# Keeping a block inverse by columns: a DeltaNet mixer's 32x32 inversion on VectorE, and what its copy-out holds

## The chip, the cores and the metric

One core of one Trainium2 chip runs the whole program. The metric is the device time of one execution in microseconds (us), median over runs of the same kernel.

## The reference, cut to what matters

The program is a two-layer decoder trunk on 512 tokens of width 1024. Each layer is a SwiGLU half step, a token mixer and another SwiGLU half step. Layer 0's mixer (the "even" one) joins eight sliding-window attention heads with four gated DeltaNet heads; layer 1's is a Mamba-2 scan. The change touches the DeltaNet heads alone. Per chunk they need a unit lower triangular solve:

```python
a_mat = jnp.where(strict, jnp.einsum('bnhid,bnhjd->bnhij', k_beta, kc) * decay, 0.0)
t_mat = a_mat + jnp.eye(B_CHUNK, dtype=a_mat.dtype)
u = lax.linalg.triangular_solve(t_mat, vc * bc, left_side=True, lower=True, unit_diagonal=True)
w = lax.linalg.triangular_solve(t_mat, k_beta * jnp.exp(g_cum)[..., None], ...)
```

(`g_cum` stands here for the cumulated log decay.) All is float32.

## The kernel before, in words

**Matrix products** are the bulk. A float32 product is made of three TensorE passes over parts split in two (high and low): lines L167, L168 and L169 for the projections of the even mixer, so 24 matmuls of 128x512 for one projected tile of 128 columns (8 steps of depth by 3). They gather in one of two PSUM banks of the tag `mm`. The weights of one such tile come by a DMA (L85, on SyncE), are cast by ScalarE (`whi`, L80) and their rest is taken by VectorE (`wlo`, L81).

**The even mixer** (`even_mixer`) runs two generators against each other: `gated_delta` (the DeltaNet heads) and `attention`, whose steps are drawn in between as filling. A scheduler that sorts by program order and readiness then fixes one order of instructions for each engine, and on the chip each engine works through its list in that order. In `gated_delta` the order of the program is: `keys` for four heads, the first half of `invert32`, `queries` for four heads, the second half of `invert32`, `values` for four heads, then the chain that puts the 32x32 blocks together (L769 to L779, on the tiles `U`, `kT` and `h`), and the recurrence.

**The inversion** (`invert32`, L695 to L727) inverts 64 blocks of 32x32 (four on the diagonal of each of 16 matrices), which go through DRAM scratch `ablk` so that each of the 128 partitions holds one block and builds 16 columns of its inverse. `nb` is the negated block (a buffer of the tag `U`, of which there are two, each 128x1024), `tb` the inverse as it grows (one of the two buffers of the tag `feat`), `pr` a scratch for products. Forward substitution takes 31 steps; step i is a VectorE product (L720) of n times m elements and a VectorE sum over m (L721), with n = min(i, 16) and m = i up to 15 and i + 1 from 16 on. Each needs the one before it. In `nb` two neighbours in m lie 32 floats apart, and in `tb` 16 floats apart. At the end one DMA writes `tb` to DRAM scratch `tblk` (L722), and eight DMAs bring the blocks back in place, into `h` (L725).

**The values** (`values(h)`, L729) take one projected tile in an `mm` bank and put it through `conv_silu`: ScalarE's copy with a factor out of PSUM (L474), three VectorE steps that still read the `mm` bank (L478), ScalarE's tanh into a scratch (L480), VectorE's last product (L481). TensorE then transposes the result (L645), and VectorE scales it (L731). The tile on which L474 to L481 work has the tag `feat`.

**The scratch**: `self.scratch()` draws from one pool with the tag `scr` and two buffers of 128x512 float32. `pr`, the tanh outputs of `conv_silu`, the DMA'd rows in `queries` and others draw from it. A buffer is given again when its last reader is done, in the order of the requests in the program.

**Attention**: the score products of a block of 128 queries (L833, L834 into a `tr` bank), VectorE's masked maximum (L838), ScalarE's exponential (L840), VectorE's reciprocal (L841), ScalarE's scaling (L842), TensorE's transposes (L849), the split (`PTh` by ScalarE, `PTl` by VectorE, L80 and L81), for each head eight products with the values (L855), a copy (L858) and a sum (L860).

Of the kernel before, what the change touches and what calls it, by code (L numbers as in the profile page):

```python
# [13 lines left out]
AF = mybir.ActivationFunctionType  # L14
OP = mybir.AluOpType
# [15 lines left out]
class Trunk:  # L31
# [542 lines left out]
    def even_mixer(self, w_in, conv_w, a_log, dt_bias, head_norm_w, w_out, post_w, next_pre):  # L574
        nc, tc = self.nc, self.tc
# [6 lines left out]
        tt, stt = nc.vector.tensor_tensor, nc.vector.scalar_tensor_tensor  # L582
        with ExitStack() as ctx:
# [52 lines left out]
            def t4(name, bufs=HB):  # L636
                return gp.tile([128, TT, 128], F32, name=name, bufs=bufs)

            def two(name):
                return gp.tile([128, 2 * TT, 128], F32, name=name, bufs=2)  # L640
# [54 lines left out]
            def invert32():  # L695


                nb = two("U").rearrange("p a b -> p (a b)").rearrange("p (j i) -> p j i", i=32)
                tb = t4("feat", 2).rearrange("p c t -> p (c t)").rearrange("p (i c) -> p i c", c=16)
                ablk = self.dram.tile([4, HB * TT, 32, 32], F32, name="ablk")  # L700
                tblk = self.dram.tile([2, 4, HB * TT, 32, 16], F32, name="tblk")
                for b in range(4):
                    s = slice(32 * b, 32 * b + 32)
                    nc.sync.dma_start(ablk[b].rearrange("q j i -> j q i"), AT[s, :, s])
                nc.gpsimd.memset(Tm, 0.0)
                nc.gpsimd.memset(tb, 0.0)
                for e in range(2):
                    half = slice(64 * e, 64 * e + 64)
                    nc.sync.dma_start(nb[half], ablk.rearrange("b q j i -> (b q) j i"))
                    nc.gpsimd.memset(tb[half, 16 * e:16 * e + 16, :].rearrange("p a b -> p (a b)")[:, ::17], 1.0)  # L710
                yield
                pr = self.scratch()
                nc.scalar.activation(nb, nb, AF.Copy, scale=-1.0)

                nc.gpsimd.memset(nb.rearrange("p a b -> p (a b)")[:, 16 * 33::33], 1.0)
                for i in range(1, 32):
                    n, m = min(i, 16), i + (i >= 16)
                    q = pr[:, :n * m].rearrange("p (c m) -> p c m", c=n)
                    a = nb[:, :m, i:i + 1].rearrange("p m o -> p o m").to_broadcast([128, n, m])
                    tt(q, a, tb[:, :m, :n].rearrange("p m c -> p c m"), op=OP.mult)  # L720
                    nc.vector.tensor_reduce(tb[:, i, :n], q, axis=mybir.AxisListType.X, op=OP.add)  # L721
                nc.sync.dma_start(tblk.rearrange("e b q i c -> (e b q) i c"), tb)  # L722
                for e in range(2):
                    for b in range(4):
                        nc.sync.dma_start(Tm[32 * b:32 * b + 32, :, 32 * b + 16 * e:32 * b + 16 * e + 16],  # L725
                                          tblk[e, b].rearrange("q i c -> i q c"))
                yield  # L727
# [24 lines left out]
            def gated_delta():  # L752
                heads = range(HB)
                K = []
                for h in heads:
                    K.append(keys(h, first[h]))
                    yield 4
                inv = invert32()
                next(inv)
                Q = []  # L760
# [467 lines left out]
```

## Time and profile before

| what | value |
|---|---|
| runs | 2144.21, 2144.45, 2148.64 us; median 2144.45 us |
| the profiled execution | 2145.76 us, of which the span of its instructions is 2144.0 us |
| mean granted TensorE clock | 0.998 |
| TensorE (PE) | 2108.8 us busy, 98% of the span |
| VectorE (DVE) | 1472.2 us busy, 69% |
| ScalarE (ACT) | 1042.0 us busy, 49% |
| GpSimd (POOL) | 149.4 us busy, 7% |
| the inversion, first product to last sum | 487.74 to 551.44 us in the span |

An engine's busy time says how much of the span it has instructions in work; where TensorE is at 98%, the time is the sum of its work and of the few places where it stands. Such a place is told by a row's bracket, "[1.94 <-DVE h L860]": 1.94 us without work before this instruction, ended by VectorE's write of `h` in line 860. Busy time at a lower granted clock is busy time as well, so the clock is read beside it.

### The profile page before, as it was taken

The numbers are of one execution on the slowest core, as the hardware profiler recorded it, in microseconds if no ns is written. First come the engines' busy times: TensorE is split into PE (matmuls) and PEld (weight loads), VectorE is DVE, ScalarE is ACT, GpSimd is POOL, SyncE is SP. The second block draws the span as 40 slices with busy tenths as digits, with TensorE's granted clock in tenths as the row PEclk, the third lists the DMA queues.
The fourth block names the chain that finished last, engine by engine and source line by source line (L and its number), as shares of the span: only waits on it lengthen the run. The fifth ranks groups of instructions, "written<-read, shape, count | busy, mean of one in ns | idle before, by whom it ended". The sixth has DMA issues, their size and how long they took to land.

```text
span 2144.0 us, 33124 instructions
## 1 busy us (share of the span) xinstructions
PE 2108.8 (98%) x13311; PEld 1869.5 (87%) x13311; DVE 1472.2 (69%) x2329; ACT 1042.0 (49%) x1613; POOL 149.4 (7%) x142
## 2 busy tenths in 40 slices
PE   8999999999999999999999999999999999999998
PEld 7999988887788999988899998887778788999986
DVE  5867656869667776656686765668888846867653
ACT  4555543555563455544345554357565423555541
POOL 0011000111200011000001000000000000011000
PEclk9999999999999999999999999999999999999999
DMA  8587324442323587533657742333333236587321
GB/s 236 145 199 163 124 95 133 109 119 68 94 70 118 148 201 176 135 128 99 158 136 184 172 128 99 101 84 100 108 108 101 78 118 157 141 197 162 122 91 67
DMA packets 284037, 277.06 MB, mean 129 GB/s; under 512 B 18576, under 2 KB 244552, under 8 KB 283884
## 3 DMA queue, kind: packets, MB, share of 16 engines
q1 hardware_dynamic: 243308, 228.81, 35.2%
q0 software_dynamic: 40576, 46.14, 12.8%
q8 instruction: 104, 1.70, 0.3%
q14 instruction: 49, 0.40, 0.1%
HBM read 265.93 MB, written 4.79 MB: 126 GB/s over the span
## 4 chain that ended last, share of the span: by engine, by line
PE 86%; DVE 6%; ACT 3%; DMA 3%; issue 2%; POOL 0%; SPq 0%; DVEq 0%; ACTq 0%; POOLq 0%
PE mm L300 19%; PE acc L300 14%; PE acc L236 10%; PE acc L235 10%; PE acc L237 10%; PE mm L167 4%; PE mm L168 4%; PE mm L169 4%; DMA M<-rows_o 2%; PE acc L651 1%; PE acc L169 1%; PE acc L168 1%; PE acc L167 1%; PE tr L154 1%; DVE wlo L81 1%
## 5 line engine op out<-in xcount | busy, mean ns | idle before, releaser
L80 ACT CAST whi<-wraw 128x1024 fp32r<-128x1024 f32 x296 | 310.1, 1049 | 392.8 <-PE acc L237 116.6
L81 DVE TENSOR_TENSOR wlo<-wraw,whi 128x1024 fp32r<-128x1024 f32 x292 | 356.8, 1223 | 154.9 <-ACT whi L80 153.1
L167 PE MATMUL mm<-uhi,whi 128*128 128x512 f32 (+1 forms) x712 | 264.7, 373 | 2.1 <-DVE feat L478 1.3
L168 PE MATMUL mm<-ulo,whi 128*128 128x512 f32 (+1 forms) x712 | 262.7, 369 | 0.3 <-DVE ulo L81 0.3
L169 PE MATMUL mm<-uhi,wlo 128*128 128x512 f32 (+1 forms) x712 | 262.9, 369 | 0.0
L80 ACT CAST whi<-wq 128x1024 fp32r<-128x1024 f32 x144 | 150.8, 1049 | 223.3 <-issue 83.2
L81 DVE TENSOR_TENSOR wlo<-wq,whi 128x1024 fp32r<-128x1024 f32 x144 | 175.2, 1220 | 83.7 <-ACT whi L80 83.6
L235 PE MATMUL acc<-whi,hs 128*128 128x512 f32 x576 | 227.3, 395 | 0.0
L236 PE MATMUL acc<-wlo,hs 128*128 128x512 f32 x576 | 227.2, 395 | 0.0
L380 POOL DMA_DIRECT2D wq<-in_ffn_w_up_dram x72 | 92.7, 1291 | 1071.0 <-DVE wlo L81 316.6
L300 PE MATMUL mm<-ulo,whi 128*128 128x256 f32 x576 | 163.0, 283 | 0.0
L300 PE MATMUL mm<-uhi,wlo 128*128 128x256 f32 x576 | 163.0, 283 | 0.0
L300 PE MATMUL mm<-uhi,whi 128*128 128x256 f32 x576 | 163.0, 283 | 0.0
L300 PE MATMUL acc<-uhi,whi 128*128 128x256 f32 x576 | 162.8, 283 | 0.0
L300 PE MATMUL acc<-uhi,wlo 128*128 128x256 f32 x576 | 162.8, 283 | 0.0
L300 PE MATMUL acc<-ulo,whi 128*128 128x256 f32 x576 | 162.8, 283 | 0.0
L167 PEld LDWEIGHTS mm<-uhi,whi 128*128 128x128 f32 x712 | 134.5, 189 | 27.8 <-issue 4.2
L168 PEld LDWEIGHTS mm<-ulo,whi 128*128 128x128 f32 x712 | 134.8, 189 | 23.5 <-issue 4.1
L169 PEld LDWEIGHTS mm<-uhi,wlo 128*128 128x128 f32 x712 | 134.7, 189 | 22.9 <-issue 3.4
L237 PE MATMUL acc<-whi,hs 128*128 128x512 f32 x384 | 151.5, 395 | 0.0
L236 PEld LDWEIGHTS acc<-wlo,hs 128*128 128x128 f32 x576 | 108.5, 188 | 25.3
L235 PEld LDWEIGHTS acc<-whi,hs 128*128 128x128 f32 x576 | 108.5, 188 | 25.1
(394 smaller groups left out, 5296.8 us busy)
## 6 DMA issues: line engine op xcount, KB each, us to landing
wraw<-in_ffn_w_down_dram SPq DMA_DIRECT2D x88, 512.0 KB, 3.5
wq<-in_ffn_w_gate_dram SPq DMA_DIRECT2D x72, 512.0 KB, 5.3
wq<-in_ffn_w_up_dram POOLq DMA_DIRECT2D x72, 512.0 KB, 8.1
wraw<-in_ffn_w_gate_dram SPq DMA_DIRECT2D x52, 512.0 KB, 6.2
wraw<-in_ffn_w_up_dram SPq DMA_DIRECT2D x52, 512.0 KB, 6.9
wraw<-in_odd_w_in_dram SPq DMA_DIRECT2D x40, 512.0 KB, 3.9
wq<-in_ffn_w_up_dram SPq DMA_DIRECT2D x36, 512.0 KB, 3.8
wraw<-in_even_w_in_dram SPq DMA_DIRECT2D x28, 512.0 KB, 4.2
```

The costliest lines, as they stand in the source:

```text
L80: nc.scalar.copy(hi, src)
L81: (nc.gpsimd if on_pool else nc.vector).tensor_tensor(lo, src, hi.bitcast(F32), op=OP.subtract)
L154: nc.tensor.transpose(p[:, j * 128:(j + 1) * 128], u[:, k * 128:(k + 1) * 128], self.ident)
L167: nc.tensor.matmul(p, whi[:, k, :], hi, start=k == 0, stop=False)
L168: nc.tensor.matmul(p, whi[:, k, :], lo, start=False, stop=False)
L169: nc.tensor.matmul(p, wlo[:, k, :], hi, start=False, stop=k == KD - 1)
L235: nc.tensor.matmul(p, ahi, hi, start=k == 0, stop=False)
L236: nc.tensor.matmul(p, ahi, lo, start=False, stop=False)
L237: nc.tensor.matmul(p, alo, hi, start=False, stop=k == nk - 1)
L300: self.nc.tensor.matmul(p[:, f * 256:(f + 1) * 256].rearrange("p (t c) -> p t c", c=128), l, r, start=new and f == k == i == 0, stop=f == ...
L380: nc.gpsimd.dma_start(raw, src, accum_op=OP.add)
L651: nc.tensor.matmul(p[:, c, :], lhs[:, c, :], rhs[:, c, :], start=True, stop=True)
```

## The change

In `invert32` the block is read from DRAM into a first `U` buffer `na`; ScalarE's negation (L713 before, L715 after) reads it transposed and writes `nb`, the second `U` buffer, so that m runs contiguously in it. `tb` keeps the inverse by columns (c, then i), so m runs contiguously there too, and the sums are written 32 floats apart. Before the DMA to `tblk` the inverse is brought back into rows by a ScalarE copy (new L724) into a new tile `out`, drawn from `self.scratch()`. Lines behind L697 are 1 to 3 higher in the changed kernel.

```diff
-                nb = two("U").rearrange("p a b -> p (a b)").rearrange("p (j i) -> p j i", i=32)
-                tb = t4("feat", 2).rearrange("p c t -> p (c t)").rearrange("p (i c) -> p i c", c=16)
+                na = two("U").rearrange("p a b -> p (a b)").rearrange("p (j i) -> p j i", i=32)
+
+                nb = two("U").rearrange("p a b -> p (a b)").rearrange("p (i j) -> p i j", j=32)
+                tb = t4("feat", 2).rearrange("p c t -> p (c t)").rearrange("p (c i) -> p c i", i=32)
...
-                    nc.sync.dma_start(nb[half], ablk.rearrange("b q j i -> (b q) j i"))
-                    nc.gpsimd.memset(tb[half, 16 * e:16 * e + 16, :].rearrange("p a b -> p (a b)")[:, ::17], 1.0)
+                    nc.sync.dma_start(na[half], ablk.rearrange("b q j i -> (b q) j i"))
+                    nc.gpsimd.memset(tb[half].rearrange("p c i -> p (c i)")[:, 16 * e::33], 1.0)
                 yield
                 pr = self.scratch()
-                nc.scalar.activation(nb, nb, AF.Copy, scale=-1.0)
+                nc.scalar.activation(nb, na.rearrange("p j i -> p i j"), AF.Copy, scale=-1.0)
 
                 nc.gpsimd.memset(nb.rearrange("p a b -> p (a b)")[:, 16 * 33::33], 1.0)
                 for i in range(1, 32):
                     n, m = min(i, 16), i + (i >= 16)
                     q = pr[:, :n * m].rearrange("p (c m) -> p c m", c=n)
-                    a = nb[:, :m, i:i + 1].rearrange("p m o -> p o m").to_broadcast([128, n, m])
-                    tt(q, a, tb[:, :m, :n].rearrange("p m c -> p c m"), op=OP.mult)
-                    nc.vector.tensor_reduce(tb[:, i, :n], q, axis=mybir.AxisListType.X, op=OP.add)
-                nc.sync.dma_start(tblk.rearrange("e b q i c -> (e b q) i c"), tb)
+                    tt(q, nb[:, i:i + 1, :m].to_broadcast([128, n, m]), tb[:, :n, :m], op=OP.mult)
+                    nc.vector.tensor_reduce(tb[:, :n, i], q, axis=mybir.AxisListType.X, op=OP.add)
+                out = self.scratch().rearrange("p (i c) -> p i c", c=16)
+                nc.scalar.copy(out, tb.rearrange("p c i -> p i c"))
+                nc.sync.dma_start(tblk.rearrange("e b q i c -> (e b q) i c"), out)
```

The change moves instructions on three engines. ScalarE's list before, at the first of the four values' tanh (L480), with the attention's steps around it:

```order
L80 CAST PTh<-tr 128x4x128
L842 ACTIVATE P<-P,aden 128x128
L480 ACTIVATE scr<-feat 128x512
L80 CAST whi<-wraw 128x1024
L858 COPY P<-tr 64x512
L474 ACTIVATE feat<-mm,cw 128x512
L80 CAST PTh<-tr 128x128
L840 ACTIVATE P,aden<-P,amax 128x256
```

ScalarE's list in the changed kernel, at the new copy L724 (`scr<-feat` is `out<-tb`):

```order
L845 ACTIVATE P<-P,aden 128x512
L80 CAST PTh<-tr 128x4x128
L861 COPY P<-tr 64x512
L724 COPY scr<-feat 128x512
L480 ACTIVATE scr<-feat 128x512
L474 ACTIVATE feat<-mm,cw 128x512 x2
L480 ACTIVATE scr<-feat 128x512 x2
L80 CAST whi<-wraw 128x1024
```

The first tanh of the values stood ahead of two more attention blocks; it now stands right behind the copy L724, and the others behind it. VectorE's list before, at the first value's last product (L481):

```order
L720 TENSOR_TENSOR scr<-U,feat 128x49
L115 TENSOR_TENSOR rs_t<-rs_y 128x16
L481 SCALAR_TENSOR_TENSOR feat<-scr,feat 128x512
L721 TENSOR_REDUCE feat<-scr 128x7
L116 TENSOR_TENSOR rs_t<-rs_t,rs_x 128x16
L720 TENSOR_TENSOR scr<-U,feat 128x64
```

VectorE's list in the changed kernel, at the inversion's end:

```order
L721 TENSOR_TENSOR scr<-U,feat 128x496
L722 TENSOR_REDUCE feat<-scr 128x16
L721 TENSOR_TENSOR scr<-U,feat 128x512
L722 TENSOR_REDUCE feat<-scr 128x16
L481 SCALAR_TENSOR_TENSOR feat<-scr,feat 128x512
L478 SCALAR_TENSOR_TENSOR feat<-mm,cw,feat 128x511
L478 SCALAR_TENSOR_TENSOR feat<-mm,cw,feat 128x510
L734 TENSOR_TENSOR vt<-acc,kl 128x512
```

The product L481 stood between step 7's product and sum; it now stands behind the last sum. TensorE's list before, at the first value's transposes (L645), with a score product ahead of them and a projection behind:

```order
L855 MATMUL tr<-PTl,va 128x128
L833 MATMUL tr<-k_4862,q_4766 128x256
L834 MATMUL tr<-k,q 128x256
L645 MATMUL acc<-ident,feat 128x128 x4
L167 MATMUL mm<-uhi,whi 128x512
L168 MATMUL mm<-ulo,whi 128x512
```

TensorE's list in the changed kernel, at the same transposes:

```order
L836 MATMUL tr<-k_4863,q_4767 128x512
L837 MATMUL tr<-k,q 128x512
L852 MATMUL tr<-ident,P 128x128 x7
L858 MATMUL tr<-PTh,va 128x512
L858 MATMUL tr<-PTl,va 128x512
L858 MATMUL tr<-PTh,va 128x384
...
L645 MATMUL acc<-ident,feat 128x128 x4
L167 MATMUL mm<-uhi,whi 128x512
L168 MATMUL mm<-ulo,whi 128x512
```

The transposes of the first value have moved behind the rest of this attention head (three more score blocks, all transposes and the products with the values) and behind the 24 matmuls of the third value's projection, which followed it before.

## Rows read from the trace of the kernel before

**Rows 1.** The page's busy times: engine, us, share of the span, instructions.
```profile
PE 2108.8 (98%) x13311; PEld 1869.5 (87%) x13311; DVE 1472.2 (69%) x2329; ACT 1042.0 (49%) x1613; POOL 149.4 (7%) x142
```

**Rows 2.** Busy time by stretch: us, each engine's busy time (instructions), granted clock, DMA.
```profile
500.00:520.00 20.00, 17.35 (x83) 13.02 (x82) 19.10 (x45) 9.77 (x19) 1.48 (x1) 1.00 0.19 52
520.00:540.00 20.00, 19.18 (x120) 16.90 (x119) 19.87 (x31) 5.83 (x9) 2.70 (x2) 1.00 0.45 124
540.00:560.00 20.00, 17.69 (x93) 14.01 (x92) 16.48 (x35) 10.46 (x24) 4.26 (x3) 1.00 0.40 95
```

**Rows 3.** TensorE's waits from 498 to 700 us: us in total, times, longest.
```profile
PE tr L849 <- ACT P L842: 2.3, 1, 2.3
PE tr L849 <- DVE h L860: 1.9, 1, 1.9
PE mm L167 <- DVE feat L478: 1.3, 2, 0.7
PE acc L651 <- ACT kT L776: 0.6, 1, 0.6
```

**Rows 4.** VectorE's groups from 487 to 552 us: busy us, mean ns | idle before.
```profile
L720 DVE TENSOR_TENSOR scr<-U,feat 128x1 f32<-128x1 f32 (+30 forms) x31 | 18.7, 604 | 0.2
L721 DVE TENSOR_REDUCE feat<-scr 128x1 f32<-128x1 f32 (+30 forms) x31 | 12.4, 399 | 0.2
L478 DVE SCALAR_TENSOR_TENSOR feat<-mm,cw,feat 128x511 f32<-128x511 f32 (+2 forms) x12 | 8.9, 738 | 0.0
L81 DVE TENSOR_TENSOR wlo<-wraw,whi 128x1024 fp32r<-128x1024 f32 x7 | 8.5, 1217 | 0.0
L838 DVE CUSTOM_DVE_ANT_0 P<-tr,abias 128x384 f32<-128x384 f32 (+3 forms) x8 | 3.8, 478 | 0.8 <-PE tr L834 0.8
L81 DVE TENSOR_TENSOR PTl<-tr,PTh 128x256 fp32r<-128x256 f32 (+3 forms) x7 | 3.6, 512 | 0.2 <-ACT PTh L80 0.2
L119 DVE TENSOR_TENSOR rs_y<-rs_t,rs_y 128x16 f32<-128x16 f32 x1 | 2.2, 2204 | 0.0
```

**Rows 5.** VectorE's timeline at two products and sums: start us, us [idle before].
```profile
498.86 0.27 DVE L720 TENSOR_TENSOR scr<-U,feat 128x64 f32<-128x64 f32 x1
499.17 0.22 DVE L721 TENSOR_REDUCE feat<-scr 128x8 f32<-128x64 f32 x1
...
549.42 1.03 DVE L720 TENSOR_TENSOR scr<-U,feat 128x512 f32<-128x512 f32 x1
...
550.76 0.68 DVE L721 TENSOR_REDUCE feat<-scr 128x16 f32<-128x512 f32 x1
```

**Rows 6.** ScalarE's timeline: the first tanh and a copy.
```profile
497.35 0.62 ACT L480 ACTIVATE scr<-feat 128x512 f32<-128x512 f32 x1
...
562.18 0.58 ACT L858 COPY P<-tr 64x512 f32<-64x512 f32 x1 [2.13 <-PE tr L855]
```

**Rows 7.** VectorE's timeline, the first value's last product.
```profile
498.03 0.68 DVE L481 SCALAR_TENSOR_TENSOR feat<-scr,feat 128x512 f32<-128x512 f32 x1
```

**Rows 8.** TensorE's timeline: the first value's transposes, attention's transposes, projections.
```profile
499.60 0.66 PE L645 MATMUL acc<-ident,feat 128*128 128x128 f32 x4
...
515.76 0.93 PE L849 MATMUL tr<-ident,P 128*128 128x128 f32 x7
...
519.89 0.48 PE L167 MATMUL mm<-uhi,whi 128*128 128x512 f32 x1
...
523.40 0.39 PE L855 MATMUL tr<-PTh,va 128*128 128x512 f32 x1
...
524.50 0.27 PE L855 MATMUL tr<-PTl,va 128*128 128x128 f32 x1
```

**Rows 9.** Busy time and granted clock around two places where TensorE stood.
```profile
417.40:419.90 2.50, 0.19 (x2) 0.00 (x0) 2.50 (x3) 2.11 (x9) 1.86 (x1) 1.00 0.74 171
419.90:424.00 4.10, 4.06 (x21) 4.06 (x22) 3.81 (x21) 0.00 (x0) 0.00 (x0) 0.58 0.93 236
...
500.00:503.00 3.00, 1.18 (x7) 0.66 (x5) 2.90 (x5) 0.69 (x1) 1.48 (x1) 1.00 0.07 9
```

## The prediction

> **What bounds the kernel now.** I read the page's busy times first. TensorE is busy for 2108.8 of 2144.0 us [rows 1], so VectorE's 1472 us only count where TensorE stands waiting for it. Then the stretch of the inversion by twenties: VectorE is full there (19.10 and 19.87 of 20 us), yet TensorE still does 17.35 and 19.18 of 20 [rows 2]. TensorE's waits from 498 to 700 us are 2.3, 1.9, 1.3 and 0.6 us, 6.1 in all [rows 3], and no wait on a product or sum of the inversion is among them. So the inversion (18.7 us of products, 12.4 us of sums, spread over 64 us [rows 4]) lies beside other work, and making it shorter can return no more than those 6.1 us. What counts is what the change does to the orders that TensorE, ScalarE and VectorE work through.
>
> **Part 1, the layout (a gain for VectorE).** In before a sum, whose input is contiguous, takes 0.22 us for 64 elements and 0.68 for 512; a product takes 0.27 and 1.03 [rows 5]. That is 1.03 ns an element on 0.155 us for the contiguous form, and 1.70 ns an element for the strided one. A contiguous VectorE operation with two inputs agrees: 1024 elements in 1.217 us [rows 4] against 1.21 by this line. I price the new products at the contiguous line. The reads gain (1.70 - 1.03) ns an element. The sums now write 16 results 128 bytes apart; the trace shows no such write, the nearest is the strided product's surcharge of 0.67 ns, times 16 is 0.01 us a sum, so I take nothing (upper bound 31 times 0.01 = 0.3 us). The Trainium skill ("SBUF — State Buffer", Door 1, the note on cachelines) says that each access that crosses to a new 16-byte line pays a penalty. By that the strided products are dear, as rows 5 show, but the new scattered sums and the copy's strided read pay too, which speaks against this change; it would leave my sum as it stands, since both are inside the bounds given here.
>
> **Part 2, the new scratch (the step that decides).** `out` comes from the two-buffer pool `scr`. `pr` holds one buffer for the whole inversion. Before, the other one went round among the values' tanh outputs, and so the first L480 ran at 497.35 us [rows 6], L481 at 498.03 [rows 7], TensorE's transposes at 499.60 [rows 8], in the middle of the inversion. Now `out` is asked for ahead of the values, takes that other buffer, and is written only when the inversion is over. All four tanh outputs come behind it. The orders show it: L480 right behind the copy L724 on ScalarE, L481 behind the last sum on VectorE. TensorE works in order, and its transposes L645 stand behind only what is left of one attention head and one projection. The values that have been projected hold both `mm` banks, so no projection can stand ahead of them either.
>
> When does the inversion end? Up to 498.0 us I leave the course as it is, with seven steps done. Steps 8 to 31 have 1100 + 6272 = 7372 elements in the products and as many in the sums: 14744 times 1.03 ns is 15.2 us, 48 times 0.155 is 7.4, and the 0.04 us between a product's end and its sum's start (499.13 to 499.17 [rows 5]) 48 times is 1.9: 24.5 us. Attention's and the queries' remaining VectorE work falls in between: three maxima at 0.48, four `PTl` at 0.51, two L860 of the 0.68 us of a 128x512 operation (as L481 [rows 7]), a `wlo` at 1.22, the slow L119 at 2.2 [rows 4] and some 0.8 us of small ones: 9.0, of which I take 8.0 as added, since neighbours that don't depend on each other overlap a little. So it ends at 498.0 + 24.5 + 8.0 = 530.5 us, 21 earlier than before's 551.4. Then come the copy, L480 and L481, one after the other. The copy L724 is new: its lower bound is a contiguous ScalarE copy, 0.58 us [rows 6]; its upper bound that of a tanh of 0.62 us stretched as strided products are, 1.03/0.68, so 0.94. I take 0.65, near the copy. With 0.62, 0.68 and 0.15 for hand-overs, L645 starts at 532.6 us.
>
> What does TensorE do from about 501.0, where it first stands in before as well, to 532.6? By its order: 18 products at (523.40 - 519.89)/15 = 0.234 us, 4.2; ten transposes at 0.93/7, 1.3; eight products with the values, 523.40 to 524.77, 1.4; four score products at the 0.39 of a 512-wide one, 1.6 [rows 8]; 0.3 for changes between them. That is 8.8 of 31.6 us: **22.8 us idle**.
>
> **Part 3, what is late next.** Behind these transposes stands the last value's projection, and it needs an `mm` bank, free only after the second value's three L478: 3 times 0.738 [rows 4] is 2.2, with a hand-over **2.3 us**. The projections of the last value, of `q` and `k` then run on end, but attention's fill has been spent, so the chain that joins the blocks is covered thinly: each of the four heads may show the wait of 0.6 us for ScalarE's `kT` [rows 3], so 0 to 2.4, and I take **2.0**. The last attention head has no other work beside it at its end. Before, one link of such a head stood bare for 2.3 us [rows 3], so one to four links cost 2.3 to 9.2 us; I take two and 0.9 for the rest, **5.5**. The DMAs to `tblk` and back into `h` start 20 us earlier than before and no one waits for them.
>
> **Part 4, TensorE's clock.** Where TensorE stood at 417.4 to 419.9 (0.19 us of work in 2.50), the granted clock was 0.58 in the next 4.1 us, part of them at the lower level, 1.2 GHz; where it stood about 1.9 us at 501 to 503, it stayed at 1.00 [rows 9]. A loss is therefore 4.1 times 0.42 = 1.7 us where it comes. Idle of 22.8 us in pieces, and a tail, may give none to four of those (0 to 7 us); I take two, **3.4 us**.
>
> **The sum.** Idle 22.8 + 2.3 + 2.0 + 5.5 = 32.6, less the 6.1 of before that this stretch takes up, plus 3.4: +29.9 us. The profiled execution took 2145.76 us (span 2144.0), 1.3 above the median of the runs; with the change it would take 2175.7, and a run by the median 2144.45 + 29.9 = **2174.4 us**.
>
> **Rivals.**
> - *Faster: VectorE's relief reaches TensorE.* If the tanh outputs don't queue behind `out` (were a third buffer free in time), the inversion's shorter operations let L860 and L478 come sooner, and the 6.1 us of waits go: 2144.45 - 6.1 = 2138.3 us. It decides from the point where L645 starts before TensorE has run through its 8.8 us, at about 510. For it speaks that VectorE is full there [rows 2]; against it, the three orders, and an inversion that can't end before 522 even without other work. 4 in 100, with 2 in 100 for a half of it that can't be told from no change (0.2%, 4.3 us, is about what a measurement of this kernel can tell).
> - *The layout doesn't do what it says.* If a broadcast operand, not the stride, makes products slow, the 7372 elements stay at 1.70 ns: 4.9 us later, 2179.3 us. For it: both versions broadcast one operand, and no product of before is contiguous. Against: the slope of 1.70 has no counterpart in other two-input operations. 12 in 100.
> - *The clock stays low.* If TensorE, after so long a stop and with work in pieces, is at 0.58 not for 4 but for some 25 us more, it loses 25 times 0.42 = 10.5 us: 2184.9 us. For it, the row at 419.9; against it, the row at 500, where the clock stayed at 1.00 through the stop, and the projections of 24 matmuls each that run on end soon after L645. 10 in 100. The Trainium skill ("TensorE: Matmul & The Clock Gate", Part 1) calls the throttled clock the default, which activity releases; by that, thin work in the stop would keep it low for longer, which is this case, and the row at 0.58 agrees so far.
> - *Later parts give it back.* If the chain and the tail stay covered by the projections and by next weights' work, 2.0 and 5.5 go, and one clock loss: 2174.4 - 9.2 = 2165.2 us. 10 in 100.
>
> **How the numbers follow.** The forecast itself has 62 in 100, with 2168 to 2180 from its bounds (copy +0.3, tail -3.2 to +3.7, clock -3.4 to +3.6, chain -2.0 to +0.4, not all at one end). The range takes in later parts that give back, with a shorter tail, down to 2160, and the low clock up to 2187; outside lie the faster rival and the ends of these, some 15 in 100. Faster by over 0.2%: 0.04; within: 0.02; slower: 0.94.
>
> **What would show it.** Right: L724 behind the last sum at about 530, L645 at about 532 with over 10 us of TensorE's idle ended by VectorE's `feat` of L481; a product of 512 at about 0.69 us; the stretch 500 to 540 with some 24 us less TensorE work than before. Wrong: L480 while the inversion runs; a product of 512 still at 1.03; a TensorE stop that ends with another releaser, or a time below 2155 us, which would mean that TensorE had work which I haven't seen in its order.

## The result, and the profile after

The changed kernel takes 2184.93 us (median of 4 runs, 2183.19 to 2187.97) against 2144.7 us before: a ratio of 1.0178, with a 95% interval from 1.0167 to 1.019. That is 40.2 us slower, inside the range that was forecast (2160 to 2187), 10.5 us above the forecast of 2174.4 and above the 2168 to 2180 that the forecast's own bounds gave. The profiled execution is the one of 2183.19 us, with a span of 2181.4, 37.4 us above before's 2144.0.

The page's busy times of the changed kernel, as in [rows 1]:

```profile
PE 2117.4 (97%) x13311; PEld 1873.1 (86%) x13311; DVE 1473.3 (68%) x2329; ACT 1044.8 (48%) x1614; POOL 148.9 (7%) x142
```

TensorE does the same 13311 matmuls. It is busy 8.6 us longer (2117.4 - 2108.8), and its idle time, the span less the busy time, is 64.0 us instead of 35.2: 28.8 more. The two make up the 37.4. VectorE's total is no smaller either: its groups add up to some 3 us less (1564.8 against 1568.1), but fewer of its instructions overlap now.

TensorE's waits of the changed kernel from 480 to 740 us, as in [rows 3]:

```profile
PE acc L645 <- DVE feat L481: 17.3, 1, 17.3
PE tr L852 <- ACT P L845: 6.6, 3, 2.4
PE mm L198 <- DVE q L81: 2.0, 1, 2.0
PE mm L167 <- DVE feat L478: 1.8, 1, 1.8
PE tr L852 <- DVE h L863: 1.7, 1, 1.7
PE tr L858 <- ACT PTh L80: 1.4, 2, 0.7
PE tr L925 <- DVE h L863: 1.2, 1, 1.2
PE tr L852 <- DVE amax L841: 1.0, 1, 1.0
```

One wait of 17.3 us stands at the top: the first value's transposes L645 for VectorE's L481. How it comes about is read from three timelines of the changed kernel, VectorE's, ScalarE's and TensorE's (columns as in [rows 5]):

```profile
530.80 0.69 DVE L721 TENSOR_TENSOR scr<-U,feat 128x512 f32<-128x512 f32 x1
531.53 0.69 DVE L722 TENSOR_REDUCE feat<-scr 128x16 f32<-128x512 f32 x1
533.93 0.69 DVE L481 SCALAR_TENSOR_TENSOR feat<-scr,feat 128x512 f32<-128x512 f32 x1 [1.71 <-ACT scr L480]
```

```profile
532.30 1.06 ACT L724 COPY scr<-feat 128x512 f32<-128x512 f32 x1 [14.36 <-DVE feat L722]
533.27 0.62 ACT L480 ACTIVATE scr<-feat 128x512 f32<-128x512 f32 x1
```

```profile
516.91 0.41 PE L858 MATMUL tr<-PTl,va 128*128 128x128 f32 x1
534.67 1.11 PE L645 MATMUL acc<-ident,feat 128*128 128x128 f32 x4 [17.34 <-DVE feat L481]
537.58 0.77 PE L167 MATMUL mm<-uhi,whi 128*128 128x512 f32 x1 [1.79 <-DVE feat L478]
538.14 0.63 PE L168 MATMUL mm<-ulo,whi 128*128 128x512 f32 x1
```

The last sum ends at 532.22, the copy into `out` runs from 532.30, the tanh L480 right behind it (in before it ran at 497.35 [rows 6]), then L481, then L645. ScalarE had stood 14.36 us ahead of the copy, TensorE 17.34 ahead of the transposes. The products did get their price: 0.69 us at 512 elements, against 1.03 [rows 5].

The busy times of the changed kernel by stretches (columns as in [rows 2]; the ninth is the granted clock):

```profile
500.00:505.00 5.00, 3.25 (x13) 1.85 (x12) 4.63 (x10) 1.21 (x4) 2.03 (x1) 1.00 0.33 87
505.00:509.70 4.70, 4.70 (x20) 3.39 (x20) 4.42 (x14) 2.87 (x6) 0.00 (x0) 1.00 0.06 19
509.70:517.40 7.70, 4.58 (x16) 3.21 (x15) 6.62 (x14) 2.82 (x7) 0.00 (x0) 0.68 0.24 68
517.40:534.60 17.20, 0.00 (x0) 0.00 (x0) 14.19 (x23) 2.82 (x4) 0.00 (x0) 0.50 0.02 8
534.60:543.30 8.70, 6.84 (x20) 5.32 (x21) 6.40 (x11) 1.96 (x4) 0.00 (x0) 0.51 0.36 45
543.30:620.00 76.70, 76.60 (x541) 68.23 (x540) 33.98 (x82) 36.04 (x86) 18.11 (x15) 1.00 0.22 64
...
627.00:634.00 7.00, 1.98 (x9) 0.97 (x9) 5.84 (x14) 6.66 (x16) 0.00 (x0) 0.85 0.62 198
634.00:640.00 6.00, 6.00 (x17) 4.73 (x18) 0.69 (x1) 0.06 (x1) 0.00 (x0) 0.60 0.89 249
640.00:680.00 40.00, 35.89 (x162) 26.27 (x161) 23.36 (x58) 23.03 (x50) 0.00 (x0) 0.96 0.21 66
```

Idle is the length of a stretch less TensorE's busy time. Up to 534.60 it is 1.75 + 3.12 + 17.20 = 22.1 us, then 1.9 before the bank comes free, 0.1 in the next 76.7, and 5.0 + 4.1 = 9.1 from 627 to 680: 33.2 in all. In before TensorE stands for 6.7 us from 500 to 700 (193.33 of 200 us busy; the 6.1 of [rows 3] are the four largest rows of its waits). Behind the stops the clock is low: 0.68, 0.51 and 0.60 in the rows at 509.70, 534.60 and 634, and 0.96 in the longer row at 640.

### The profile page after: what moved, and what is told of

Read it like the earlier page. It is cut to its first block, busy times and chain, and to the rows that moved or that the text cites. A ratio compares the mean times of both kernels' runs of the same rounds, so it can differ in the third digit from the quotient of the medians.

```text
span 2181.4 us, 33133 instructions
## 1 busy us (share of the span) xinstructions
PE 2117.4 (97%) x13311; PEld 1873.1 (86%) x13311; DVE 1473.3 (68%) x2329; ACT 1044.8 (48%) x1614; POOL 148.9 (7%) x142
## 4 chain that ended last, share of the span: by engine, by line
PE 87%; DVE 5%; ACT 4%; DMA 2%; issue 2%; POOL 0%; SPq 0%; DVEq 0%; ACTq 0%; POOLq 0%
PE mm L300 19%; PE acc L300 14%; PE acc L235 9%; PE acc L236 9%; PE acc L237 9%; PE mm L167 5%; PE mm L168 5%; PE mm L169 5%; DMA M<-rows_o 1%; PE acc L651 1%; PE acc L169 1%; PE acc L168 1%; PE acc L167 1%; PE tr L154 1%; ACT M L1098 1%
```

## The experiments

### Where `out` lives: two kernels with the layout and without the held scratch

```diff
-                out = self.scratch().rearrange("p (i c) -> p i c", c=16)
+                out = na.rearrange("p j i -> p (j i)")[:, :512].rearrange("p (i c) -> p i c", c=16)
```

> The changed kernel with one edit: `out` is a view of the first half of `na`, the U buffer that is dead after the negation, instead of a new tile from `scr`. Layout, copy and DMA stay. Theory (the held scratch makes the stop): the values' L480 run in the middle of the inversion again, the 17.3 us wait of L645 on L481 is gone, the two-input products stay contiguous (0.69 us at 512), and the time is 2138 to 2147 us (at most the 6.1 us of TensorE's waits below before's 2144.7). Rival (the new layout, its transposed negation or the strided copy is what costs): it stays above 2170 us. Rival (the stop is only half the cost, the thin tail the other): about 2160 us.

```diff
-                out = self.scratch().rearrange("p (i c) -> p i c", c=16)
+                out = pr.rearrange("p (i c) -> p i c", c=16)
```

> The changed kernel with the smallest edit: `out` is a view of `pr`, the products' own scratch, which is dead behind the last sum; no further scratch is asked for. Theory (held scratch): as with the dead U buffer, 2138 to 2147 us; the two differ by under 2 us, since only the DMA to DRAM holds the buffer and no value waits for it. Rival (layout or copy costs): above 2170 us.

With `out` in the dead buffer of `U`: 2142.57 us, a ratio to before of 0.9981 [0.9972, 0.999]. With `out` in `pr`: 2142.01 us, 0.9979 [0.997, 0.9988]. Before's median beside them is 2146.18 us, of 21 runs, and the ratios here go by that. One changed line takes the 40 us away and leaves a kernel that is faster than before by 0.2%. Of the second, ScalarE's timeline, then VectorE's last product and sum, then TensorE's waits from 498 to 760 us:

```profile
498.40 0.62 ACT L480 ACTIVATE scr<-feat 128x512 f32<-128x512 f32 x1
...
548.16 1.13 ACT L724 COPY scr<-feat 128x512 f32<-128x512 f32 x1
```

```profile
545.67 0.69 DVE L721 TENSOR_TENSOR scr<-U,feat 128x512 f32<-128x512 f32 x1
546.73 0.68 DVE L722 TENSOR_REDUCE feat<-scr 128x16 f32<-128x512 f32 x1
```

```profile
PE tr L852 <- DVE h L863: 1.8, 1, 1.8
PE tr L925 <- DVE og L921: 0.2, 1, 0.2
PE tr L852 <- ACT P L845: 0.2, 1, 0.2
```

L480 runs at 498.40 again, 50 us ahead of the copy, which is now in no one's way. Of before's waits [rows 3] the 2.3 (for ScalarE's P), the 1.3 (for L478) and the 0.6 are gone, 4.2 us, and the span fell by 3.8 (2144.0 to 2140.2). So the layout does relieve VectorE, and what reaches TensorE is bounded by its waits, as the prediction's first paragraph had it; the two rivals of this experiment, that the layout costs or that half of the cost stays, are out.

### The order of the requests alone

```diff
+                yield
                 out = self.scratch().rearrange("p (i c) -> p i c", c=16)
...
                 vt = [values(h) for h in heads]
+                next(inv)
```

> The changed kernel with one yield more: the inversion's generator stops behind the last sum, the four values are asked for, and only then `out`, the copy and the DMA are. Buffers, layout and copy are those of the changed kernel; only the order of the requests on the pool differs. Theory (it is the order of requests on a pool of two): the tanh outputs take their buffers first, L480 runs in the middle of the inversion, and the time is that of the runs without the extra scratch, 2140 to 2145 us; the copy L724 may come some us later, since it waits for the last tanh's buffer, and nothing on TensorE waits for that. Rival (a pool of two is too small for an `out` of its own wherever it is asked for): above 2150 us.

2142.64 us, 0.9979 [0.997, 0.9989]; before's median beside it, as beside the run with 188 matmuls and the two half layouts below, is 2146.72 us, of 25 runs; the other experiments go by 2146.18. L480 runs at 499.06 and the copy at 550.44. The pool, its two buffers, `out` as a tile of its own and the copy are all those of the changed kernel. A pool of two is enough; what made the stop is that `out` was asked for ahead of four tiles that are needed earlier. Whether a pool of three would do as well isn't shown: a third buffer takes 2 KB more per partition, and the pool `normp` would then find 27.72 KB per partition where it needs 28, so the kernel does not fit in this form.

### The held scratch without the layout

```diff
-                nc.sync.dma_start(tblk.rearrange("e b q i c -> (e b q) i c"), tb)
+                out = self.scratch().rearrange("p (i c) -> p i c", c=16)
+                nc.scalar.copy(out, tb)
+                nc.sync.dma_start(tblk.rearrange("e b q i c -> (e b q) i c"), out)
```

> The kernel before with the scratch alone added: strided products and rows as before, and behind the last sum `out` = self.scratch(), a ScalarE copy (here contiguous) and the DMA from `out`. Theory: the stop of TensorE is there without the new layout, and longer by what the strided products take more (18.7 - 14.7 = 4.0 us by the two traces) less some 0.4 us of the cheaper copy: L645 waits some 20 to 21 us, and the time is 2187 to 2192 us, above the changed kernel's 2184.9. Rival (layout costs): it is near before, below 2155 us.

2186.73 us, 1.0185 [1.0172, 1.0199]. In this kernel three lines stand for one of before and nothing else differs, and the whole loss is there. Its TensorE waits, the first row from 498 to 760 us, and its copy:

```profile
PE acc L645 <- DVE feat L481: 19.7, 1, 19.7
```

```profile
536.48 0.62 ACT L723 COPY scr<-feat 128x512 f32<-128x512 f32 x1 [17.18 <-DVE feat L721]
```

The time is a little under the expected 2187 to 2192, and the wait a little under 20 to 21 us; by the spans this kernel is 3.2 us longer than the changed one (2184.6 and 2181.4), and 2.4 of them are the longer wait for L481 (19.7 and 17.3). That is where strided products should tell, since VectorE is the one waited for; but the runs' intervals overlap, so the difference rests on one profile each and is not shown by the times.

### What the low clock costs: two fillings of the stop

```diff
+                d = self.ps("acc")
+                self.tc.cur_priority += 2000
+                for _ in range(150):
+                    x = self.ident.bitcast(BF16)
+                    nc.tensor.matmul(d[:, :256], x[:, :128], x, start=True, stop=True)
+                self.tc.cur_priority -= 2000
                 out = self.scratch().rearrange("p (i c) -> p i c", c=16)
```

> The changed kernel with 150 added matmuls of the identity (128x256, bf16, result unread) that TensorE's order places where it would stand before L645: 22 ahead of the last four transposes of the head, 11 around its first products, 117 behind them. Nothing waits for them but TensorE's own order. Theory (part of the cost is the lower clock after the stop, some 8.6 us of busy time in all by the two traces, about 6 of it around this stop): the granted clock from 518 to 543 us is at 1.00 instead of 0.50, the matmuls 128x512 behind L645 go 0.23 us apart instead of 0.43, and the time falls by 3 to 6 us to 2179 to 2182 us; the wait for L481 itself doesn't get shorter. Rival (the clock costs nothing that isn't hidden by VectorE's conv steps of the values): 2183 to 2187 us.

2187.61 us, 1.0185 [1.0169, 1.02]: a miss. TensorE's timeline tells why:

```profile
518.39 12.95 PE L727 MATMUL acc<-ident 128*128 128x256 bf16 x117
535.92 1.11 PE L645 MATMUL acc<-ident,feat 128*128 128x128 f32 x4 [4.59 <-DVE feat L481]
539.88 0.76 PE L167 MATMUL mm<-uhi,whi 128*128 128x512 f32 x1 [2.84 <-DVE feat L478]
540.44 0.63 PE L168 MATMUL mm<-ulo,whi 128*128 128x512 f32 x1
540.87 0.63 PE L169 MATMUL mm<-uhi,wlo 128*128 128x512 f32 x1
```

The added matmuls ended 4.59 us ahead of L645, another 2.84 stood empty behind it, and the projection began with matmuls 0.43 us apart, at half speed, as in the changed kernel. This execution was also a microsecond late at the attention's first transposes behind 500 us (504.54, in the changed kernel 503.54), and its clock was at 0.55 from 506.50 to 510.00, where the changed kernel's was at 1.00. So this run said nothing on the clock, and the next one used 188 of them (range(188) in the same diff).

> As the run with 150 added matmuls, but 188: in TensorE's order 33 stand in the stops of the attention head, 134 (17 more than before) in the long stop ahead of L645 and 21 between L645 and the projection that waits for an mm bank. With 150 the matmuls ended 4.6 us ahead of L645 and 2.8 us without work came behind it, and the clock was at 0.50 again until 543 us; so that run did not tell what the clock costs. Theory (the low clock behind the stop costs some 2.5 us there): now under 3 us stay empty ahead of L645 and under 1 us behind, the matmuls behind L645 go 0.23 us apart from the start instead of 0.43, and the time is 2 to 4 us below that run's 2187.6. Rival (the empty 2 to 3 us are still enough to lose the clock, or VectorE's conversions of the values hide it): within 1 us of it.

2182.91 us, 1.0167 [1.0152, 1.0182]. TensorE's timeline:

```profile
518.62 14.80 PE L727 MATMUL acc<-ident 128*128 128x256 bf16 x134
536.15 0.66 PE L645 MATMUL acc<-ident,feat 128*128 128x128 f32 x4 [2.73 <-DVE feat L481]
536.65 4.10 PE L727 MATMUL acc<-ident 128*128 128x256 bf16 x21
540.40 0.60 PE L167 MATMUL mm<-uhi,whi 128*128 128x512 f32 x1
540.84 0.39 PE L168 MATMUL mm<-ulo,whi 128*128 128x512 f32 x1
541.07 0.40 PE L169 MATMUL mm<-uhi,wlo 128*128 128x512 f32 x1
...
553.03 0.66 PE L645 MATMUL acc<-ident,feat 128*128 128x128 f32 x4
```

And its busy times and clock behind L645:

```profile
536.80:540.40 3.60, 3.60 (x23) 2.58 (x20) 3.50 (x7) 1.32 (x2) 0.00 (x0) 0.56 0.48 46
```

The clock fell here too, behind the 2.73 us that stayed empty (0.56), but it was the 21 added matmuls that ran at it. The matmuls of the projection are at their full rate almost from the start (0.23 us apart from 540.84). From the projection's first matmul to the last value's transposes this kernel takes 553.03 - 540.40 = 12.6 us; the changed kernel takes 15.1 for the same work (537.58 to its L645 at 552.69). So the low clock behind this stop costs 2.5 us, as the theory said. The whole time fell by 4.7 us against the run with 150, more than the 2 to 4 expected, but against the changed kernel itself the intervals overlap: this execution was 1.2 us late at the same transposes (504.73), its clock too was low from 506.50 to 510.00 (0.51), and the 21 matmuls behind L645 held the projection until 540.40 (537.58 in the changed kernel). It is a measurement of the clock, not a remedy. The long stop didn't get shorter: L645 still came at 536.

### Which operand's stride makes the product dear

Half the layout each: `nb` contiguous with `tb` in rows (no `out`), and `tb` by columns with `nb` as before (`out` in `pr`). The core of each against the kernel before:

```diff
-                    a = nb[:, :m, i:i + 1].rearrange("p m o -> p o m").to_broadcast([128, n, m])
+                    a = nb[:, i:i + 1, :m].to_broadcast([128, n, m])
                     tt(q, a, tb[:, :m, :n].rearrange("p m c -> p c m"), op=OP.mult)
```

> Half of the layout: the negation reads transposed into a second U buffer, so nb is contiguous in m; tb stays in rows (16 floats apart), no `out`, no copy. Theory (each strided operand adds to the price): the product of 512 takes between the 0.69 us of two contiguous operands and the 1.03 of two strided ones, about 0.86. Rivals: one strided operand costs as much as two (1.03, time as before, 2144 to 2148), or only the broadcast one matters (0.69, time 2141 to 2143).

```diff
-                    a = nb[:, :m, i:i + 1].rearrange("p m o -> p o m").to_broadcast([128, n, m])
-                    tt(q, a, tb[:, :m, :n].rearrange("p m c -> p c m"), op=OP.mult)
-                    nc.vector.tensor_reduce(tb[:, i, :n], q, axis=mybir.AxisListType.X, op=OP.add)
+                    tt(q, nb[:, :m, i:i + 1].rearrange("p m o -> p o m").to_broadcast([128, n, m]), tb[:, :n, :m], op=OP.mult)
+                    nc.vector.tensor_reduce(tb[:, :n, i], q, axis=mybir.AxisListType.X, op=OP.add)
```

> The other half: tb by columns, contiguous in m, with the copy into pr behind the last sum; nb as before, 32 floats apart, negated in place. Theory (each strided operand adds): about 0.86 us for the product of 512. Rivals: 1.03 (one strided operand is enough) or 0.69 (the broadcast operand's stride is free). Time 2141 to 2147 us in each case, since the inversion lies beside other work.

Both take the time of before: 1.0 [0.9991, 1.0009] and 1.0002 [0.9992, 1.0011]. The last product of the first, then of the second kernel, on VectorE's timeline, with the second one's last sum:

```profile
552.06 1.02 DVE L721 TENSOR_TENSOR scr<-U,feat 128x512 f32<-128x512 f32 x1
```

```profile
550.17 1.01 DVE L719 TENSOR_TENSOR scr<-U,feat 128x512 f32<-128x512 f32 x1
551.51 0.67 DVE L720 TENSOR_REDUCE feat<-scr 128x16 f32<-128x512 f32 x1
```

My theory that each strided operand adds to the price is wrong. One is enough (1.01 or 1.02 us, whichever it is), and only with both contiguous does it fall to 0.69. The broadcast operand counts like the other, and a contiguous broadcast adds nothing to the 0.69, so the prediction's rival that the broadcast makes products slow is out. So the change's two halves give nothing one by one, and all of their gain together. The sum that writes 16 results 128 bytes apart costs 0.67 to 0.69 us, as the 0.68 of [rows 5].

## Why the prediction was right, and where its sizes were off

The way and the mechanism were right, and the range held the time. The time lies outside the forecast's own bounds (2168 to 2180), though, in the part of the range that was taken in for a low clock. By its steps:

- **Layout (part 1)**: a contiguous product was priced by the sums' line, 0.69 us at 512; measured 0.69. The 31 products take 12.5 us in the kernel with `out` in `pr`, against 18.7 [rows 4]; in the changed kernel it is 14.7, mostly since one of them was held up by 2.0 (last section). The scattered sums were priced at nothing; measured at nothing. The Trainium skill ("SBUF — State Buffer", Door 1, the note on cachelines) says that each access which crosses to a new 16-byte line pays a penalty. The runs agree for the products with either operand strided and for the copy. On the sums' writes these runs can't tell: at the surcharge of part 1, 16 of them come to 0.01 us, less than the scatter from 0.67 to 0.69.
- **The held scratch (part 2)**: L480 behind the copy, the inversion's end at 530.5 (532.2 measured), L645 at 532.6 (534.7), 22.8 us idle up to it (22.1). The last of these agrees better than its parts: L645 came 2.1 us later, but TensorE's own work took 11.6 us instead of 8.8, as the low clock stretched it (the row at 509.70 has 4.58 us of work where 2.3 were forecast). For the same reason TensorE's busy time from 500 to 540 fell by 20.5 us (36.53 to 16.07), not by some 24. The run of the hold alone shows that it is the cause and that the layout isn't. Within this step the copy was mis-sized: 1.06 us against the 0.65 taken and an upper bound of 0.94. That bound came from VectorE's ratio of strided to contiguous, 1.5; on ScalarE the contiguous copy of this shape takes 0.62 (the run of the hold alone) and the strided read 1.06 to 1.15 (from the changed kernel to the one with `tb` alone by columns), so 1.7 to 1.9.
- **What is late next (part 3)**: the `mm` bank 2.3 (1.9). The thin chain was taken at 2.0 and showed 0.1 us: the projections covered it. The last attention heads were taken at 5.5 us and cost 9.1, near the upper bound of 9.2 given there. The waits from 620 to 700 us tell how: 5.9 in the heads themselves (L852 for ScalarE's P 4.2 and for `amax` 1.0, L858 for PTh 0.7), and 3.2 for which part 3 had no term (L198 for the `mm` bank that the split of q reads, 2.0, and L925 for the `tr` bank that the last head's sum reads, 1.2). Chain and tail were 7.5 together in the sum and 9.2 in the trace. The rival that later parts give it back is therefore out.
- **The clock (part 4)** is the term with the largest miss: 3.4 us taken, 8.6 us of longer busy time measured, above the 7 us that the part gave as its upper end. I counted two stretches of 1.7 us; the rows show four places. The one at 509.70 has 2.2 us more work than forecast, the one at 534.60 has 6.84 us at 0.51, a loss of 3.4, the one at 634 has 6.00 at 0.60, a loss of 2.4, and the one at 640 has 35.89 at 0.96, a loss of 1.4: 9.4 in all. The place by which the term was priced, 0.58 from 419.9 to 424.0 [rows 9], lost nothing in the changed kernel's execution: TensorE stood there for the same instruction as long (L198, 2.38 us against 2.35 in before), and the clock was at 1.00 behind it, which gives 1.7 back; 0.9 of the 8.6 stay without a place. So a stop of this length does not lose the clock in every execution, and the 8.6 us are those of one. The rival of a low clock didn't come as it was told: it had some 25 us at 0.58 behind the stop, and the clock is at 1.00 in the row from 543.30 to 620. That the median fell on this rival's 2184.9 us is chance.
- **The sum**: the terms of idle time come to 32.6 us in the forecast and 33.2 in the trace, less 6.1 and 6.7 that before has there, so 26.5 on either side. That they agree so closely is in part luck: the chain was 1.9 too much, the tail 3.6 too little, and part 2's errors cancel as told above. Another 2.3 us of idle lie outside this stretch, 1.5 of them ahead of 500 us and 0.8 behind 700, for which the forecast had no term. With the clock 29.9 were forecast and 37.4 measured between the spans; the medians are 40.2 apart, since before's profiled execution lay 1.1 us above its median and the changed kernel's 1.7 below.
- **The rival on the other side**, that VectorE's relief reaches TensorE, was right about its worth and about its condition: where the tanh outputs don't queue behind `out`, the kernel takes 2142.0 to 2142.6 us, against 2146.2 and 2146.7 of before beside these runs. It had taken all 6.1 us for it; 4.2 were found.

## What to carry to other kernels

A tile that is asked for from a rotating pool takes its buffer at the place of the request in the program, not when it is written: asked for ahead of tiles that are needed earlier, it holds them all back, and through in-order engines that becomes a stop (17.3 us here, with 9.1 of thin tail and 8.6 of low clock behind it, for a copy of 1.06 us). Before adding a scratch tile, list who draws from the pool behind it, and use a buffer that is dead by then, or move the request. And a two-input product with inputs 64 or 128 bytes apart, as here, is worth making contiguous only if both inputs are.

## What the runs showed of the hardware that I had not expected

- One strided input makes a VectorE product of float32 as slow as two: 1.02 and 1.01 us at 128x512 against 1.03, and 0.69 with none. It made no difference whether the strided one was broadcast.
- The slow L119 of before (2.2 us for 128x16 [rows 4]) was not slow by itself. In the changed kernel the same line took 0.17 us, and a product of 100 elements that should take 0.26 took 2.27. GpSimd, which does some of the splits of weight tiles (`wlo`), was at one both times. VectorE's and GpSimd's timelines there, of before:

```profile
499.31 2.20 DVE L119 TENSOR_TENSOR rs_y<-rs_t,rs_y 128x16 f32<-128x16 f32 x1
```

```profile
499.11 2.37 POOL L81 TENSOR_TENSOR wlo<-wraw,whi 128x1024 fp32r<-128x1024 f32 x1 [7.47 <-ACT whi L80]
```

and of the changed kernel, with an earlier place:

```profile
417.96 2.34 DVE L116 TENSOR_TENSOR rs_t<-rs_t,rs_x 128x4 f32<-128x4 f32 x1
...
499.21 0.17 DVE L119 TENSOR_TENSOR rs_y<-rs_t,rs_y 128x16 f32<-128x16 f32 x1
...
499.88 2.27 DVE L721 TENSOR_TENSOR scr<-U,feat 128x100 f32<-128x100 f32 x1
```

```profile
417.18 3.10 POOL L81 TENSOR_TENSOR wlo<-wraw,whi 128x1024 fp32r<-128x1024 f32 x1 [24.11 <-ACT whi L80]
...
499.65 2.38 POOL L81 TENSOR_TENSOR wlo<-wraw,whi 128x1024 fp32r<-128x1024 f32 x1 [7.45 <-ACT whi L80]
```

In the changed kernel GpSimd's split of a weight tile ends at 502.03, the product at 502.15; in before the split ends at 501.48, L119 at 501.51. At the earlier place the split ends at 420.28, and L116, with 4 elements, at 420.30. Each time the VectorE product caught beside the split lasts until about its end, whichever it is. Not every VectorE operation is caught: beside a split from 462.68 to 465.08 in the changed kernel a reciprocal took its 0.16 us and a `PTl`, one of whose two inputs lies in PSUM, its 0.56. That a product of two inputs from SBUF, the on-chip memory of the tiles, can't go on beside the split is what these rows suggest; no run was made to test it. The prediction's 2.2 us were right in size and booked to the wrong line.
